# Forming half of the low weight parts with ScalarE and an accumulating DMA in both MLPs' first matrix

## The chip, the cores and the metric

The kernel runs on one core of one Trainium2 chip. The metric is device microseconds of one execution, from its first to its last instruction with the launch's own small overhead; two executions of the kernel before took 2568.08 and 2568.37 us, median 2568.22 us. Profiles are taken separately: one execution, recorded by the hardware.

The engines in the text are TensorE (PE in profile rows; its weight loads are PEld), VectorE (DVE), ScalarE (ACT), GpSimd (POOL) and the DMA queues that SyncE (SP) and GpSimd issue to. All DMA queues share the core's 16 DMA engines.

## The reference

A trunk of two layers on one sequence of 256 tokens, model width 2048, float32. Layer 0 is a retention layer, layer 1 is a latent attention (MLA) layer; each is followed by the same kind of MLP:

```python
def sq_relu_mlp(h, w1, w2):
    return jnp.square(jax.nn.relu(h @ w1)) @ w2

def reference(x, positions, ...):
    for layer in range(DEPTH):          # DEPTH = 2
        h = rms_norm(x, norm_mix[layer])
        if layer < N_A_LAYERS:          # layer 0
            x = x + retention(h, ...)
        else:                           # layer 1
            x = x + mla_attention(h, ...)
        x = x + sq_relu_mlp(rms_norm(x, norm_mlp[layer]), mlp_w1[layer], mlp_w2[layer])
    return x
```

The two matrices of an MLP are 2048 x 8192 (`w1`) and 8192 x 2048 (`w2`): 67 MB each in float32, so the two MLPs read 268 MB of the 470 MB that the kernel reads in all.

## The kernel before

**Two parts of a number.** Every product is made of three. A float32 matrix is split into a high part of 12 bits (`wh`, type fp32r) and a low part `wl = w - wh`; so are the activations. TensorE then adds high times high, high times low and low times high. `split` (L128) makes the parts: ScalarE copies the source into the high part, which rounds it (L131), and VectorE subtracts the rounded part from the source (L132).

**The stream of weights.** `stream` (L154) takes one chunk of a matrix, at most 128 partitions x 2048 float32, 1024 KB (1.05 million bytes). SyncE loads it into a buffer `raw`, of which there are three (L158). Each half of the chunk, 128 x 1024, is then split into one `wh` and one `wl` tile, of which there are five each; and `use` issues the matmuls on the half. The tile framework puts in the waits: a load waits until everything that read the `raw` buffer three chunks earlier is done, a split waits until TensorE is done with the tiles of five halves earlier.

**The first matrix of an MLP.** `gemm_t` (L201) makes 256 columns of `w1`, transposed, out of two chunks. For each block of 128 rows and each 128 columns it issues two matmuls: the low part of the weights against the 256 tokens' high activation (L216, 128 x 256), and the high part against the tokens' high and low activations side by side (L220, 128 x 512). After the second chunk `up` (L544) takes the 256 columns out of PSUM: ScalarE copies (L548), VectorE adds and applies relu and the norm's scale (L549, L551), ScalarE squares (L552), and a `split` makes the two parts of the hidden activations. The 8192 hidden features are made in three groups (of 12, 10 and 10 calls of `gemm_t`), and after each group the rows of `w2` that belong to it are multiplied in `gemm` (L191 to L194; three matmuls of 128 x 512 for each block). In profile rows the tiles of the first matrix are called `u_raw`, `u_wh`, `u_wl`, those of the second `d_raw`, `d_wh`, `d_wl`. One layer has 64 chunks of `u` and 64 of `d`.

**What sets the order.** Each engine works in the order of the program. ScalarE's queue in the first matrix has, for each chunk, two copies of a half, and after each second chunk the four steps of `up`. GpSimd's queue is empty in both MLPs but for the scales of the norm at their ends (`rstd`, L119 and L121). SyncE's queue has only the loads.

Of the kernel before, what the change touches and what calls it, by code (L numbers as in the profile page):

```python
# [15 lines left out]
AF = mybir.ActivationFunctionType  # L16
ALU = mybir.AluOpType
AX = mybir.AxisListType
PSUM = bass.MemoryType.PSUM
# [30 lines left out]
def yoco(ctx: ExitStack, tc: tile.TileContext, a):  # L50
# [19 lines left out]
        return psum.tile([P, 2, 512], F32, tag="at", bufs=1, name=name)  # L70

    def act_tile(name, dtype=F32R):
        """Two blocks of 128 features, each with its two halves (of precision, as a rule) side by side."""
        return pool.tile([P, 2, 2, S], dtype, tag="act", bufs=20, name=name)

    # Work that waits for other engines is issued some pieces of a product later.
    queue = []
    clock, count = [0], itertools.count()

# [14 lines left out]
        while len(items) < n:  # L94
            run_first()

# [1 line left out]
    gains = pool.tile([P, G_ALL], F32, name="gains")  # L98
    cst = pool.tile([P, C_ALL], F32, name="cst")
    pos_i = pool.tile([P, NT], I32, name="pos_i")  # L100
# [11 lines left out]
    def gain(col):  # L112
        return gains[:, col : col + 1]

# [1 line left out]
    def rstd(total, n, w, name):  # L116
        """(total / n + eps) ** -0.5 for [P, w] sums of squares."""
        m = small(w, f"{name}_m")
        nc.gpsimd.tensor_scalar(m, total, 1.0 / n, EPS, op0=ALU.mult, op1=ALU.add)  # L119
        r = small(w, f"{name}_r")  # L120
        nc.gpsimd.tensor_tensor(r, m, neg_half[:, :w], op=ALU.pow)  # L121
        return r
# [2 lines left out]
        junk = pool.tile([P, 512], BF16, tag="junk", bufs=2, name=f"{name}_sq")  # L125
        nc.scalar.activation(junk[:, : src.free_size()], src, AF.Square, accum_out=acc)

    def split(h, l, src, scale=None):  # L128
        """h + l = src * scale, each of 12 bits."""
        if scale is None:  # L130
            nc.scalar.copy(h, src)  # L131
            nc.vector.tensor_tensor(l, src, h.bitcast(F32), op=ALU.subtract)  # L132
        else:
            nc.scalar.activation(h, src, AF.Copy, scale=scale)  # L134
            nc.vector.scalar_tensor_tensor(
                l, src, scale, h.bitcast(F32), op0=ALU.mult, op1=ALU.subtract
            )
# [6 lines left out]
                split(v[:, j, 0], v[:, j, 1], src[:, j], scales[j])  # L144

    def transposed(srcs, name):
        """[tokens, 128] pairs of both token tiles -> [128, 2, S] in PSUM."""
        tp = bank("tp", [2, S], name)
        for j in range(2):
            for t in range(NT):  # L150
                nc.tensor.transpose(tp[:, j, t * P : (t + 1) * P], srcs(t, j), ident)
        return tp

    def stream(w, chunk, cols, name, use, done=None, before=None):  # L154
        """use(half, parts of the weights) for both halves of a chunk of the weights."""
        raw = pool.tile([P, 2048], F32, tag="raw", bufs=3, name=f"{name}_raw")
        if before is None:
            nc.sync.dma_start(raw[:, :cols], w[chunk])  # L158
        n = cols // 2
        for half in range(2):  # L160
            wh = pool.tile([P, 1024], F32R, tag="wh", bufs=5, name=f"{name}_wh{half}")
            wl = pool.tile([P, 1024], F32R, tag="wl", bufs=5, name=f"{name}_wl{half}")
            cuts = 1
            if before is not None:
                cuts = 1 if half else 2
                m = n // cuts
                for i in range(cuts):
                    lo = half * n + i * m
                    nc.sync.dma_start(raw[:, lo : lo + m], w[chunk][:, lo : lo + m])
                    if i == 0:  # L170
                        before(half)
            m = n // cuts
            for i in range(cuts):
                lo = half * n + i * m
                split(wh[:, i * m : (i + 1) * m], wl[:, i * m : (i + 1) * m], raw[:, lo : lo + m])
            use(half, wh, wl)
        if done is not None:
            queue.append((clock[0] + 1, -1, done))
        tick()

    def piece(w, chunk, acc, act, g, nk, nb, name, before=None, done=None):
        """acc[token tile] += act @ w for rows 512 * g to 512 * (g + 1)."""
        if before is None:
            need(act, 2 * g + 2)

        def use(half, wh, wl):
            for j in range(2):
                k = g * 4 + half * 2 + j
                rh, rl = (v[:, j * nb : (j + 1) * nb] for v in (wh, wl))
                for t in range(NT):  # L190
                    ah, al = (act[k // 2][:, j, i, t * P : (t + 1) * P] for i in range(2))  # L191
                    nc.tensor.matmul(acc[t], ah, rh, start=k == 0, stop=False)  # L192
                    nc.tensor.matmul(acc[t], ah, rl, start=False, stop=False)  # L193
                    nc.tensor.matmul(acc[t], al, rh, start=False, stop=k == nk - 1)  # L194

        stream(
            w, chunk, 4 * nb, f"{name}{g}", use, done and (lambda: done(acc)),
            before and (lambda half: before(2 * g + half)),
        )

    def gemm_t(w, chunk0, act, nk, name, done):  # L201
        """done(PSUM tiles [128 of 256 columns of w, (act parts h and l) @ w by token])."""
        acc = accs(512, name)
        n = nk // 8
        for g in range(n):
# [17 lines left out]
                        if k == 0:  # L223
                            low()

            stream(w, chunk0 + g, 2048, f"{name}{g}", use, (lambda: done(acc)) if g == n - 1 else None)

    def accs(nb, name):
        return [bank("acc", [nb], f"{name}_acc{t}") for t in range(NT)]

    def gemm(w, chunk0, act, nk, nb, name, done, before=None):
        """done(PSUM tiles [tokens, nb] of act @ w)."""
        acc = accs(nb, name)
        n = nk // 4
        for g in range(n - 1):
            piece(w, chunk0 + g, acc, act, g, nk, nb, name, before)
        last_piece(w, chunk0, acc, act, nk, nb, name, done, before)
# [3 lines left out]
        piece(w, chunk0 + g, acc, act, g, nk, nb, name, before, done)  # L241

    def gemm_blocks(w, chunk_of, act, nk, name, done):
        """All column blocks of 512, the first two side by side until the last rows of act."""
        n = nk // 4
        first = [accs(512, f"{name}{b}") for b in range(2)]
        for b in range(2):
            for g in range(n - 1):
                piece(w, chunk_of(b) + g, first[b], act, g, nk, 512, f"{name}{b}")
        for b in range(2):  # L250
            last_piece(w, chunk_of(b), first[b], act, nk, 512, f"{name}{b}", lambda acc, b=b: done(b, acc))
        for b in range(2, NB):
            gemm(w, chunk_of(b), act, nk, 512, f"{name}{b}", lambda acc, b=b: done(b, acc))

    def x_block_t(b, g0s, outs, name):
        """The split transposes of x's column block b, times each gain."""
        for k2 in range(2):
            tp = transposed(
                lambda t, j: x[t][b][:, (2 * k2 + j) * P : (2 * k2 + j + 1) * P], f"{name}_tp{b}{k2}"
# [20 lines left out]
    row = pool.tile([P, S], F32, name="row")  # L280

    def token_row(r, row, name):
        """row = the scales of the tokens, along every partition."""
        wide = f2k([NT, P], f"{name}_wide")
        for t in range(NT):
            nc.vector.tensor_copy(wide[:, t], r[t].to_broadcast([P, P]))
# [7 lines left out]
        later(1, turn)  # L294

    def into_next(ss, g0s, outs, r, name, row=None):
        """What follows a block of x that is complete; r gets the scales of the next norm."""

        def done(b, acc):
            add_to_x(acc, b, ss, name)  # L300
# [5 lines left out]

        return done

# [1 line left out]
    c1, c2, c3 = _pi_parts()  # L310
    pos_f = pool.tile([P, NT], F32, name="pos_f")

    def sincos(inv, w, name):
        """Makes what returns sin and cos [P, 2, NT, w] of position * inv."""
        n = NT * w
        ang = f2k([NT, w], f"{name}_ang")
        for t in range(NT):
# [70 lines left out]

        later(1, turn)

# [1 line left out]
    act0, r0, y_act, ret_sc, mla_sc = [], [], [], [], []  # L392

    def first_inputs(c):
        """The split columns 256 * c of the first norm's input."""
        t = f2k([2, S], f"x0t_{c}")
        nc.sync.dma_start(t, a["xt"][:, 2 * c : 2 * c + 2, :])
        v = act_tile(f"a0_{c}")
# [23 lines left out]
            later(20, mla_tables)  # L422

    def ret_rope(acc, out, name, wait):
        """One head's rotated q or k by feature: [128, dk half, S]."""
        u = f2k([2, S], f"{name}_u")
        for i in range(2):
            nc.scalar.copy(u[:, i], acc[i][:, S:])
# [106 lines left out]
        a["ret_w_out"], lambda b: b * 8, y_act, 32, "ro", into_next(ss, [G_MLP0], [act], r, "n1", row)  # L535
    )

# [1 line left out]
    def mlp(layer, act, row, done):  # L539
        w1, w2 = a[f"mlp_w1_{layer}"], a[f"mlp_w2_{layer}"]  # L540
        f0 = 0
        for gi, nf in enumerate(GROUPS):
# [12 lines left out]
                hid.append(v)  # L555

            for f in range(2 * f0, 2 * (f0 + nf)):
                gemm_t(w1, f * 2, act, KD, f"u{layer}_{f}", lambda acc, f=f: up(acc, f))
            for b in range(NB):

                def add(acc, b=b, last=gi == len(GROUPS) - 1):
# [10 lines left out]
    mlp(0, act, row, into_next(ss, [G_KV, G_MIX1], [act_kv, act_q], r2, "n2"))  # L572
    need(r2, 2)

# [1 line left out]
    def pe_rope(dst, u, src, t, i, heads):  # L576
        """dst = the rotation of src [P, heads, ROPE], gains in the tables."""

        def tab(j, lo, n):
            return pe_tabs[t][i][:, j, lo : lo + n].unsqueeze(1).to_broadcast([P, heads, n])  # L580
# [47 lines left out]
    for b in range(2):  # L628
        gemm(a[f"mla_w_kv_down_{b}"], 0, act_kv, KD, KV_NBS[b], f"kd{b}", lambda acc, b=b: downed(acc, b))

# [1 line left out]
    ssq = [small(3, f"ssq{t}") for t in range(NT)]  # L632
    cq, rq = [], []

# [21 lines left out]
    for b in range(3):  # L656
        gemm(a["mla_w_dq"], b * 4, act_q, KD, 512, f"dq{b}", lambda acc, b=b: queried(acc, b))

# [1 line left out]
    k_t, v_s = [], []  # L660

    def keyed(acc, b):
# [23 lines left out]
    for b in range(8):  # L686
        gemm(a["mla_w_kv_up"], b, ckv, 4, 512, f"ku{b}", lambda acc, b=b: keyed(acc, b))

# [1 line left out]
    nc.vector.tensor_scalar(gqn, gain(G_QN), scale, None, op0=ALU.mult)  # L690
    o_act = []

# [35 lines left out]
        later(3, turn)  # L728

    def score(b, qt, qpe):  # L730
        """Scores [query, head, keys of tile 0 for both query tiles, then tile 1], then softmax."""
        sc = two_banks(f"s{b}")
        for hh in range(2):
            rows = slice(hh * ROPE, (hh + 1) * ROPE)
# [145 lines left out]
```

## Time and profile before

| | |
|---|---|
| median of the executions shown | 2568.22 us |
| span of the profiled execution | 2566.0 us |
| matmul busy | 2554.7 us, 12786 matmuls |
| VectorE busy | 1475.5 us |
| ScalarE busy | 1233.7 us |
| GpSimd busy | 135.7 us |
| DMA | 473.85 MB, mean 185 GB/s |
| granted TensorE clock | 1.000 |

The profiled execution's own time is its span, 2566.0 us, with some 2 us around it up to the median of the timed executions. A row of the groups reads: line, engine, operation, output tile <- input tiles, shapes, count, then busy time and mean nanoseconds of one, then the engine's idle time before these instructions and what ended it. Matmuls are pipelined, so that the mean length of one is longer than the distance between two, and a busy TensorE is not TensorE at its peak. A DMA's row gives the time from its issue until its data has landed.

### The profile page before, as it was taken

To read this page: it belongs to the slowest core of one execution; us is meant where nothing else is said; L and a number is where in the kernel's file an instruction comes from. 1 tells how busy PE (TensorE), PEld (TensorE's weight loads), DVE (VectorE), ACT (ScalarE), POOL (GpSimd) and SP (SyncE) were. 2 spreads that over 40 slices of the span, in tenths; PEclk is the share of its full clock that TensorE was granted. 3 is DMA by queue.
4 is the path that set the end of the run, shared out by engine and by line. 5 is a ranking of instruction groups with operands and counts; after the bars stand their busy time and mean duration, and the time that the engine had idled before them with its cause. 6 is when DMAs were issued, how large, how long until landed. Compare 5 with 4: busy or idle time off the path is not lost.

```text
span 2566.0 us, 31690 instructions
## 1 busy us (share of the span) xinstructions
PE 2554.7 (100%) x12786; PEld 2168.1 (84%) x12786; DVE 1475.5 (58%) x1828; ACT 1233.7 (48%) x1651; POOL 135.7 (5%) x211
## 2 busy tenths in 40 slices
PE   8999999999999999999999999999999999999999
PEld 7888888888888888888888888998888888888887
DVE  6655555554556644654565656776666446645654
ACT  6444444443445533543454566554555435534542
POOL 6200000000000000000000002221000000000000
PEclk9999999999999999999999999999999999999999
DMA  8555555555555555555555464444455555555554
GB/s 297 182 177 180 181 181 183 182 184 186 190 183 192 183 197 194 184 188 191 196 182 196 148 221 152 148 144 148 174 188 182 196 197 181 191 190 193 184 202 140
DMA packets 71571, 473.85 MB, mean 185 GB/s; under 512 B 8192, under 2 KB 9344, under 8 KB 18176
## 3 DMA queue, kind: packets, MB, share of 16 engines
q1 hardware_dynamic: 71280, 471.78, 52.1%
q8 instruction: 100, 1.64, 0.2%
q14 instruction: 47, 0.39, 0.0%
q10 hardware_dynamic: 144, 0.05, 0.0%
HBM read 469.70 MB, written 2.10 MB: 184 GB/s over the span
## 4 chain that ended last, share of the span: by engine, by line
PE 97%; POOL 2%; DMA 0%; DVE 0%; issue 0%; SPq 0%; DVEq 0%
PE u_acc L220 19%; PE u_acc L216 9%; PE d_acc L192 9%; PE d_acc L194 9%; PE d_acc L193 9%; PE ro_acc L194 2%; PE ro_acc L193 2%; PE ro_acc L192 2%; PE rv_acc L192 2%; PE rv_acc L194 2%; PE rv_acc L193 2%; PE rk_acc L220 2%; PE rq_acc L220 2%; PE rg_acc L192 2%; PE rg_acc L194 2%; PE rg_acc L193 2%
## 5 line engine op out<-in xcount | busy, mean ns | idle before, releaser
L220 PE MATMUL u_acc<-n,u_wh 128*128 128x512 f32 x2048 | 718.1, 398 | 0.0
L216 PE MATMUL u_acc<-n,u_wl 128*128 128x256 f32 x2048 | 564.8, 281 | 0.0
L132 DVE TENSOR_TENSOR d_wl<-d_raw,d_wh 128x1024 fp32r<-128x1024 f32 x256 | 313.6, 1225 | 321.6 <-ACT d_wh L131 321.6
L220 PEld LDWEIGHTS u_acc<-n,u_wh 128*128 128x128 f32 x2048 | 381.0, 188 | 88.8
L132 DVE TENSOR_TENSOR u_wl<-u_raw,u_wh 128x1024 fp32r<-128x1024 f32 x256 | 313.3, 1224 | 241.1 <-ACT u_wh L131 241.1
L131 ACT CAST d_wh<-d_raw 128x1024 fp32r<-128x1024 f32 x256 | 269.8, 1054 | 374.0 <-PE d_acc L194 347.4
L192 PE MATMUL d_acc<-d_wh,hid 128*128 128x512 f32 x1024 | 398.6, 389 | 0.0
L194 PE MATMUL d_acc<-d_wh,hid 128*128 128x512 f32 x1024 | 398.4, 389 | 0.0
L193 PE MATMUL d_acc<-d_wl,hid 128*128 128x512 f32 x1024 | 398.4, 389 | 0.0
L131 ACT CAST u_wh<-u_raw 128x1024 fp32r<-128x1024 f32 x256 | 269.1, 1051 | 260.2 <-PE u_acc L220 210.2
L216 PEld LDWEIGHTS u_acc<-n,u_wl 128*128 128x128 f32 x2048 | 386.7, 189 | 5.6
L194 PEld LDWEIGHTS d_acc<-d_wh,hid 128*128 128x128 f32 x1024 | 192.3, 188 | 40.0
L193 PEld LDWEIGHTS d_acc<-d_wl,hid 128*128 128x128 f32 x1024 | 192.3, 188 | 39.8
L192 PEld LDWEIGHTS d_acc<-d_wh,hid 128*128 128x128 f32 x1024 | 192.3, 188 | 39.4
L132 DVE TENSOR_TENSOR ro_wl<-ro_raw,ro_wh 128x1024 fp32r<-128x1024 f32 x64 | 78.4, 1225 | 84.2 <-ACT ro_wh L131 84.2
L132 DVE TENSOR_TENSOR rg_wl<-rg_raw,rg_wh 128x1024 fp32r<-128x1024 f32 (+1 forms) x68 | 78.9, 1166 | 60.9 <-ACT rg_wh L131 60.9
L131 ACT CAST ro_wh<-ro_raw 128x1024 fp32r<-128x1024 f32 x64 | 67.4, 1053 | 94.6 <-PE ro_acc L194 86.5
L192 PE MATMUL rg_acc<-rg_wh,a 128*128 128x512 f32 x256 | 101.1, 396 | 5.7 <-ACT a L134 5.7
L132 DVE TENSOR_TENSOR rv_wl<-rv_raw,rv_wh 128x1024 fp32r<-128x1024 f32 x64 | 79.3, 1250 | 41.3 <-ACT rv_wh L131 41.3
L131 ACT CAST rg_wh<-rg_raw 128x1024 fp32r<-128x1024 f32 (+1 forms) x68 | 67.8, 998 | 72.9 <-PE rv_acc L194 46.7
L193 PE MATMUL rg_acc<-rg_wl,a 128*128 128x512 f32 x256 | 100.3, 392 | 0.2 <-DVE rg_wl L132 0.2
L192 PE MATMUL rv_acc<-rv_wh,a 128*128 128x512 f32 x256 | 100.4, 392 | 0.0
(260 smaller groups left out, 4072.5 us busy)
## 6 DMA issues: line engine op xcount, KB each, us to landing
u_raw<-in_mlp_w SPq DMA_DIRECT2D x128, 1024.0 KB, 4.8
d_raw<-in_mlp_w SPq DMA_DIRECT2D x128, 1024.0 KB, 4.8
rv_raw<-in_ret_w_gv SPq DMA_DIRECT2D x32, 1024.0 KB, 4.7
ro_raw<-in_ret_w_out SPq DMA_DIRECT2D x32, 1024.0 KB, 4.7
rg_raw<-in_ret_w_gv SPq DMA_DIRECT2D x28, 1024.0 KB, 4.7
uq_raw<-in_mla_w_uq SPq DMA_DIRECT2D x24, 768.0 KB, 4.3
rq_raw<-in_ret_w_qk SPq DMA_DIRECT2D x16, 1024.0 KB, 4.8
rk_raw<-in_ret_w_qk SPq DMA_DIRECT2D x16, 1024.0 KB, 4.7
```

Source lines behind the costliest of these rows:

```text
L131: nc.scalar.copy(h, src)
L132: nc.vector.tensor_tensor(l, src, h.bitcast(F32), op=ALU.subtract)
L192: nc.tensor.matmul(acc[t], ah, rh, start=k == 0, stop=False)
L193: nc.tensor.matmul(acc[t], ah, rl, start=False, stop=False)
L194: nc.tensor.matmul(acc[t], al, rh, start=False, stop=k == nk - 1)
L216: nc.tensor.matmul(acc[f][:, 0:S], wl[:, cols], a[:, 0], start=False, stop=False)
L220: nc.tensor.matmul(acc[f], wh[:, cols], a.rearrange("p i s -> p (i s)"), start=k == 0, stop=k == nk - 1)
```

## The change

`mlp` passes its layer's number to `gemm_t`, and this to `stream`, as `dma_low`. For the second half of each chunk of `w1`, and for nothing else, `split` then works in another way: ScalarE writes the high part as before, ScalarE writes minus the source rounded to the same type, which is minus the high part, into the low part's tile, and a DMA issued by GpSimd adds the float32 weights to that tile in place. The DMA's source is the weights in HBM in layer 0 (`dma_low` is 0, `w[chunk]`), and the `raw` buffer in SBUF in layer 1 (`dma_low` is 1). VectorE has no part in these halves any more. There are 64 such halves in each layer. Comments were taken out as well, and line numbers move by a few.

```diff
-    def split(h, l, src, scale=None):
-        if scale is None:
+    def split(h, l, src, scale=None, again=None):
+        if again is not None:
+            nc.scalar.copy(h, src)
+            nc.scalar.activation(l, src, AF.Copy, scale=-1.0)
+            nc.gpsimd.dma_start(l, again, accum_op=ALU.add)
+        elif scale is None:
             nc.scalar.copy(h, src)
             nc.vector.tensor_tensor(l, src, h.bitcast(F32), op=ALU.subtract)
...
-    def stream(w, chunk, cols, name, use, done=None, before=None):
+    def stream(w, chunk, cols, name, use, done=None, before=None, dma_low=None):
...
-                split(wh[:, i * m : (i + 1) * m], wl[:, i * m : (i + 1) * m], raw[:, lo : lo + m])
+                part = slice(lo, lo + m)
+                again = None
+                if dma_low is not None and half == 1:
+                    again = (raw if dma_low else w[chunk])[:, part]
+                split(wh[:, i * m : (i + 1) * m], wl[:, i * m : (i + 1) * m], raw[:, part], again=again)
...
-    def gemm_t(w, chunk0, act, nk, name, done):
+    def gemm_t(w, chunk0, act, nk, name, done, dma_low=None):
...
-            stream(w, chunk0 + g, 2048, f"{name}{g}", use, (lambda: done(acc)) if g == n - 1 else None)
+            stream(
+                w, chunk0 + g, 2048, f"{name}{g}", use, (lambda: done(acc)) if g == n - 1 else None, dma_low=dma_low
+            )
...
-                gemm_t(w1, f * 2, act, KD, f"u{layer}_{f}", lambda acc, f=f: up(acc, f))
+                gemm_t(w1, f * 2, act, KD, f"u{layer}_{f}", lambda acc, f=f: up(acc, f), dma_low=layer)
```

## The prediction, before the result was known

> **What bounds the kernel now.** I read the page's busy times first, then the chain that ended last, then the waits of TensorE, and then one stretch of the first matrix in order of time.
>
> ```profile
> PE 2554.7 (100%) x12786; PEld 2168.1 (84%) x12786; DVE 1475.5 (58%) x1828; ACT 1233.7 (48%) x1651; POOL 135.7 (5%) x211
> ...
> PE 97%; POOL 2%; DMA 0%; DVE 0%; issue 0%; SPq 0%; DVEq 0%
> ...
> L132 DVE TENSOR_TENSOR u_wl<-u_raw,u_wh 128x1024 fp32r<-128x1024 f32 x256 | 313.3, 1224 | 241.1 <-ACT u_wh L131 241.1
> ```
> ```profile
> PE rg_acc L192 <- ACT a L134: 5.7, 1, 5.7
> PE tr_tp L151 <- DVE tr_scaled L384: 1.1, 2, 0.7
> PE rg_acc L193 <- DVE rg_wl L132: 0.2, 1, 0.2
> ```
>
> TensorE is the bound everywhere. The chain is 97% TensorE, and the second fence is the whole list of what TensorE waited for: three entries, 7.0 us, all at the start and none in an MLP. The change can gain nothing that the chain holds: all of TensorE's idle time is 2566.0 - 2554.7 = 11.3 us. The 128 subtractions that VectorE loses (128 x 1.224 = 157 us) lie beside matmuls. So the question is only whether the new way of making a low part still arrives in time.
>
> The stretch that tells is one turn of ScalarE in the first matrix (columns: start, length, operation, idle before and its releaser):
>
> ```profile
> 1250.28 0.73 ACT L548 COPY u<-u_acc 128x256 f32<-128x256 f32 x2 [1.43 <-PE u_acc L220]
> 1250.90 1.05 ACT L131 CAST u_wh<-u_raw 128x1024 fp32r<-128x1024 f32 x1
> 1252.22 0.63 ACT L552 ACTIVATE u<-u 128x512 f32<-128x512 f32 x1 [0.27 <-DVE u L551]
> 1252.88 0.62 ACT L131 CAST hid<-u 128x512 fp32r<-128x512 f32 x1
> 1253.44 1.05 ACT L131 CAST u_wh<-u_raw 128x1024 fp32r<-128x1024 f32 x1
> 1256.26 1.05 ACT L131 CAST u_wh<-u_raw 128x1024 fp32r<-128x1024 f32 x1 [1.77 <-PE u_acc L220]
> 1259.09 1.05 ACT L131 CAST u_wh<-u_raw 128x1024 fp32r<-128x1024 f32 x1 [1.77 <-PE u_acc L220]
> 1261.56 0.73 ACT L548 COPY u<-u_acc 128x256 f32<-128x256 f32 x2 [1.43 <-PE u_acc L220]
> ...
> 1267.55 1.05 ACT L131 CAST u_wh<-u_raw 128x1024 fp32r<-128x1024 f32 x1 [1.77 <-PE u_acc L220]
> ```
>
> From 1250.28 to 1261.56 is one call of `gemm_t`, two chunks, four halves: 11.28 us, so **5.64 us for a chunk and 2.82 for a half**. The casts at 1253.44 and 1259.09 are those of second halves, which the change touches. Each starts as TensorE gives back the tile of five halves earlier, so TensorE has four halves in hand, 4 x 2.82 = 11.28 us, before it needs this one. Before the change 1.05 + 1.22 us of it are used.
>
> **The change part by part.**
>
> *ScalarE.* 128 more instructions of 128 x 1024. No row has this form; the 128 x 512 rows above give 0.63 for ACTIVATE beside 0.62 for CAST, so I take 1.07, a little over the cast's 1.05 (bounds 1.05, and twice 0.63, 1.27). 128 x 1.07 = 137 us. They lie in ScalarE's idle time: the first between 1254.49 and 1256.26 (1.77 us), the second between 1260.14 and 1261.56 (1.42 us). Were that cover gone, `up`'s copies would start a fraction of a microsecond later, against a whole call of 11.28 us until their PSUM tiles are wanted again: nothing. The second write waits for the low tile of five halves earlier, which TensorE gives back no later than the high one; behind it in ScalarE's queue stand the next cast and `up`, and they lose nothing by it.
>
> *GpSimd.* 128 issues. No row shows GpSimd issuing a DMA. The near rows:
>
> ```profile
> L158 SPq DMA_DIRECT2D u_raw<-in_mlp_w x128: 327/328/328, 728.6 to 2424.4; - x128
> ```
> ```profile
> L119 POOL TENSOR_SCALAR n_m<-n_tot 128x1 f32<-128x1 f32 x8 | 2.4, 302 | 981.4 <-DVE n_tot L270 981.0
> ...
> L327 POOL TENSOR_TENSOR tr_kl<-tr_k,tr_kh 128x512 f32<-128x512 f32 x1 | 2.4, 2369 | 0.1
> ...
> L121 POOL TENSOR_TENSOR cq_r<-cq_m,neg_half 128x1 f32<-128x1 f32 x2 | 2.1, 1044 | 0.2
> ```
>
> SyncE's issue takes 0.33 us, GpSimd's dearest single operation 2.37. I take 1.0, the price of a small GpSimd operation that does work for each partition, and keep both ends. One issue in 5.64 us fits either way. An issue that waits holds up only the issues behind it and, at the end of an MLP, the norm's scales (L119), which come after the last matrix block and so long after the last add. [...]
>
> *The add itself.* No row has an accumulating DMA. The nearest are plain loads:
>
> ```profile
> u_raw<-in_mlp_w SPq DMA_DIRECT2D x128, 1024.0 KB, 4.8
> ...
> x<-in_x SPq DMA_DIRECT2D x8, 256.0 KB, 8.6
> ...
> kd_raw<-in_mla_w_kv_down SPq DMA_DIRECT2D x4, 512.0 KB, 3.3
> ```
>
> Twice the bytes take 1.5 us more, so a load is 1.8 us and 1.5 for each 512 KB. The lower end for the add is 3.3. It must read the tile as well as the weights, twice the bytes in, and I take the 1024 KB row, **4.8**. The upper end, however far, is the slowest rate of the three rows, 8.6 for 256 KB, hence 17.2; those loads were queued behind others at the kernel's start. [...] With the write counted as a third pass the row would be 1.8 + 4.5 = 6.3, and that case is a rival below.
>
> What the 16 engines can carry is seen where loads are queued (columns: stretch, busy times, then clock, DMA share, GB/s):
>
> ```profile
> 20.00:24.00 4.00, 4.00 (x19) 3.31 (x18) 4.00 (x6) 3.28 (x7) 3.83 (x3) 1.00 1.03 416
> 24.00:28.00 4.00, 4.00 (x19) 3.16 (x18) 4.00 (x6) 2.42 (x4) 3.85 (x3) 1.00 1.02 411
> 28.00:32.00 4.00, 4.00 (x22) 3.40 (x21) 2.52 (x2) 2.15 (x6) 3.83 (x3) 1.00 1.02 412
> 32.00:36.00 4.00, 4.00 (x25) 3.45 (x24) 2.78 (x2) 4.00 (x9) 3.83 (x3) 1.00 1.02 415
> 1250.28:1306.73 56.45, 56.45 (x322) 49.04 (x321) 34.89 (x40) 30.09 (x41) 0.00 (x0) 1.00 0.53 186
> ```
>
> About 415 GB/s with the engines full, and 186 in the first matrix. With the add as two reads a chunk moves 1.05 + 1.05 = 2.10 million bytes in 5.64 us, 372 GB/s, nine tenths of 415: it fits, and load and add will overlap most of the time. Where they overlap wholly, the two take 2.10 MB / 415 GB/s = 5.05 us of data, and each lands 1.8 + 5.05 = 6.85 us after its issue.
>
> *Layer 0 (weights from HBM).* The negative is ready at 1253.44 + 1.05 + 1.07 = 1255.56. TensorE ends halves 2.82 apart, at 1250.62 (2.82 and 5.64 before the releases of 1253.44 and 1256.26), so the half five later begins at 1250.62 + 5 x 2.82 = 1264.72: a cover of **9.16 us** for issue and landing. Alone these take 1.0 + 4.8 = 5.8, fully overlapped 7.85. Hidden. The raw buffer is given back by ScalarE at 1255.56, where VectorE did it at 1253.44 + 1.05 + 1.22 = 1255.71; the next load into it is due at 1267.55, 12 us later, and even at 6.85 is in time. Without the cover a microsecond too much costs a third of one for each chunk, since the ring of five tiles comes round in three chunks: 64 / 3 = 21 us for the layer.
>
> *Layer 1 (weights from the raw buffer).* Here the buffer is held until the add has landed, and only then SyncE may load the chunk three later. The wait that is late next is SyncE's, and behind it stand all later loads. From 1255.56 to the cast of that buffer at 1267.55 is 12.0 us for add plus load: 5.8 + 4.8 = 10.6 alone, 7.85 + 6.85 = 14.7 fully overlapped. A late cast can be caught up, since the three ScalarE steps then run on end, 1.05 + 1.05 + 1.07 = 3.17; three chunks are 16.92, so add plus load may be 13.75 before TensorE pays. At 10.6 it pays nothing; at 14.7 the chunk takes (14.7 + 3.17) / 3 = 5.96, 0.32 more, 64 x 0.32 = 20 us. The engines are nine tenths full, which speaks for the late end, and a late load overlaps less, which speaks for the early one: I take the middle, **10 us**.
>
> Sum: nothing from VectorE and ScalarE, 0 in layer 0, +10 in layer 1: span 2566.0 + 10 = 2576, and with the 2.2 us that lie between span and median **2578 us**. At the issue's upper end, 2.37, layer 0 stands at its edge (9.2) and layer 1 at (16.1 + 3.17) / 3 = 6.42, +50; at the add's lower end nothing is paid, 2568.
>
> **The rivals.** About 2% (51 us) is what a measurement of this kernel can tell from no change.
>
> *The engines fill up, slower.* The place is the 16 DMA engines in the first matrix. They carry 5.64 x 415 = 2.34 MB in a chunk, so the add may cost 1.29 MB, 2.5 times its 0.524 MB. At three passes (read, read, write) a chunk is 2.62 MB, 6.32 us: 128 x 0.68 = +87, **2655 us**. At four it is 7.58, +249, 2817. For it: nothing in the trace says that an engine adds as fast as it copies. Against it: the 415 rows count a load's bytes once although it is read and written.
>
> *The add is late, with the engines not full.* If issue and landing take 12 us, layer 0's ring gives 3 chunks = 5.64 + 2.12 + 12, 6.59 for one, +61; layer 1's (12 + 4.8 + 3.17) / 3 = 6.66, +65: **2694 us**. For it: the 8.6 us of the 256 KB row, and that GpSimd's price is unknown. Against it: the 3.3 of the 512 KB row.
>
> *The freed VectorE helps.* At most TensorE's 11.3 us of idle time, which lie elsewhere: 2557.
>
> **How the numbers follow.** The forecast (0 to 50 us more, all within 2%) has 0.51, the full engines 0.28, the late add 0.20 (a quarter of it short of 51 us), the gain 0.01. That gives within 2% 0.51 + 0.05 + 0.01 = 0.57, less 0.01 kept for a gain that no row shows: 0.56; slower 0.28 + 0.15 = 0.43; faster 0.01. The range goes from 2565 to 2760: it leaves out the dearer 0.15 of the full engines and hardly anything below, and takes in the late add.
>
> **What would show it.** GpSimd's 128 issues and their landing: near 6 to 8 us, in both layers. ScalarE's new row near 1.07, VectorE's `u_wl` row with 128 instead of 256. DMA share in the first matrix near 0.9 to 1.0, with GB/s up. No wait of TensorE for the add in layer 0, a few tenths a chunk in layer 1, and there SyncE's wait ended by the add. Wrong it would be if the add lands later than 9 us even in layer 0, or if the engines' share is 1 at fewer than 372 GB/s.

## The result

The changed kernel took 2594.59 us (2589.93 and 2599.24) against 2568.22 us: a ratio of 1.0103, 95% interval 1.0084 to 1.0122. A second measurement gave 2590.05 us, 1.0088 (1.0073 to 1.0103). It is slower, by about 1%, where 2578 was forecast: the sign and the 2% bound were right, the size about two fifths of what came. The profiled execution has a span of 2597.5 us, 31.5 more than before; it is the longer of the two executions.

On the page after the change, these lines answer to those shown of before (busy times, the chain, the groups of the new low parts, the DMA queues):

```profile
PE 2562.7 (99%) x12786; PEld 2170.2 (84%) x12786; DVE 1319.6 (51%) x1700; ACT 1348.9 (52%) x1779; POOL 246.7 (9%) x339
...
q1 hardware_dynamic: 71280, 471.78, 50.3%
q0 software_dynamic: 18432, 67.12, 14.0%
...
PE 73%; issue 14%; DMA 9%; POOL 3%; ACT 1%; DVE 0%; SPq 0%; POOLq 0%; ACTq 0%; DVEq 0%
...
L132 ACT ACTIVATE u_wl<-u_raw 128x1024 fp32r<-128x1024 f32 x128 | 135.4, 1058 | 77.5 <-PE u_acc L224 60.4
...
L133 POOL DMA_DIRECT2D u_wl<-in_mlp_w x64 | 55.6, 869 | 712.5 <-ACT u_wl L132 700.3
...
L133 POOL DMA_DIRECT2D u_wl<-u_raw x64 | 55.2, 863 | 644.7 <-ACT u_wl L132 543.0
```

The pieces cost about what was put down for them: ScalarE's write 1.06 us (1.07), GpSimd's issue 0.86 (1.0), and VectorE lost 156 us of work that nobody waited for. What is new is DMA in the chain, and these waits of TensorE and of its weight loads (columns: time in all, times, longest):

```profile
PE u_acc L224 <- DMA u_wl<-u_raw: 12.2, 9, 2.9
PE u_acc L224 <- DMA u_wl<-in_mlp_w: 11.8, 14, 2.0
```
```profile
PEld u_acc L224 <- DMA u_wl<-in_mlp_w: 18.0, 20, 2.4
PEld u_acc L224 <- DMA u_wl<-u_raw: 15.9, 12, 3.2
```

TensorE waits for the add in both layers (`in_mlp_w` is layer 0, `u_raw` layer 1; the two lists overlap in time). How the loss divides is read from the tile `row`, which is written once at the start of each MLP. Before, then after:

```profile
L292 ACT COPY row<-n_rtp x2: 367/367/367, 761.0 to 1861.9; 128x256 f32<-128x256 f32 x2
```
```profile
L302 ACT COPY row<-n_rtp x2: 362/362/363, 760.5 to 1877.3; 128x256 f32<-128x256 f32 x2
```

Between the two copies lie layer 0's MLP and the attention: 1100.9 us before, 1116.8 after, +15.9. Behind the second copy lies layer 1's MLP: 704.1 us before, 720.2 after, +16.1. (The stretch ahead of the first copy is 0.5 shorter.) **Both layers pay alike** in this execution, where 0 and 10 had been forecast.

The issues and their landings (size, then median us from issue to landing):

```profile
u_raw<-in_mlp_w SPq DMA_DIRECT2D x128, 1024.0 KB, 7.9
...
u_wl<-in_mlp_w POOLq DMA_DIRECT2D x64, 512.0 KB, 10.0
u_wl<-u_raw POOLq DMA_DIRECT2D x64, 512.0 KB, 7.7
```

The add lands 10.0 us after its issue in layer 0, not 7.85 at the most. And one stretch of the first matrix in each of two groups (columns as before; the last three are clock, DMA share, GB/s):

```profile
1030.00:1120.00 90.00, 88.20 (x499) 75.83 (x498) 36.05 (x48) 61.45 (x79) 13.12 (x16) 1.00 1.00 272
```
```profile
1250.00:1260.00 10.00, 9.98 (x57) 8.41 (x57) 2.36 (x4) 6.41 (x8) 1.73 (x2) 1.00 1.02 282
1260.00:1270.00 10.00, 8.10 (x38) 6.79 (x37) 3.01 (x4) 4.29 (x6) 0.86 (x1) 0.83 1.00 273
```

The DMA engines show a share of 1.00. The second fence shows that a stall can cost twice: TensorE is idle for 1.9 us between 1260 and 1270, and its granted clock there is 0.83, which is another 1.7. In slices of 2 us the clock reads 0.91, 0.50 and 0.73 from 1262 to 1268, and 1.00 on both sides. Two waits in layer 1, of 2.9 and 2.6 us, were followed by the same drop (0.67, 0.50 and 0.98 from 2188 to 2194, and 0.84, 0.50 and 0.81 from 2416 to 2422); the other waits were not, though one of them, in layer 0, took 2.0. Each drop lost 1.7 us. Three times 1.7 are about 5 of the 31.5 us, and over the execution the clock was 0.998. What decides whether a wait is followed by a drop these traces do not tell: after 1.9, 2.6 and 2.9 us one came, after 2.0 none.

### The profile page after: what moved, and what is told of

Read it like the earlier page. It is cut to its first block, busy times and chain, and to the rows that moved or that the text cites. A ratio compares the mean times of both kernels' runs of the same rounds, so it can differ in the third digit from the quotient of the medians.

```text
span 2597.5 us, 32181 instructions
## 1 busy us (share of the span) xinstructions
PE 2562.7 (99%) x12786; PEld 2170.2 (84%) x12786; DVE 1319.6 (51%) x1700; ACT 1348.9 (52%) x1779; POOL 246.7 (9%) x339
## 3 DMA queue, kind: packets, MB, share of 16 engines
q0 software_dynamic: 18432, 67.12, 14.0%
## 4 chain that ended last, share of the span: by engine, by line
PE 73%; issue 14%; DMA 9%; POOL 3%; ACT 1%; DVE 0%; SPq 0%; POOLq 0%; ACTq 0%; DVEq 0%
PE d_acc L200 7%; PE d_acc L201 7%; PE d_acc L202 7%; PE u_acc L228 6%; DMA u_wl<-u_raw 4%; PE u_acc L224 3%; DMA u_raw<-in_mlp_w 3%; PE ro_acc L202 2%; PE ro_acc L200 2%; PE ro_acc L201 2%; PE rv_acc L200 2%; PE rv_acc L202 2%; PE rv_acc L201 2%; DMA u_wl<-in_mlp_w 2%; PE rk_acc L228 2%
## 5 line engine op out<-in xcount | busy, mean ns | idle before, releaser
L136 DVE TENSOR_TENSOR u_wl<-u_raw,u_wh 128x1024 fp32r<-128x1024 f32 x128 | 156.6, 1223 | 297.3 <-ACT u_wh L135 297.3
L132 ACT ACTIVATE u_wl<-u_raw 128x1024 fp32r<-128x1024 f32 x128 | 135.4, 1058 | 77.5 <-PE u_acc L224 60.4
L559 DVE TENSOR_TENSOR u<-u_acc,u 128x256 f32<-128x256 f32 x128 | 49.4, 423 | 158.3 <-ACT u L558 158.3
L133 POOL DMA_DIRECT2D u_wl<-in_mlp_w x64 | 55.6, 869 | 712.5 <-ACT u_wl L132 700.3
L133 POOL DMA_DIRECT2D u_wl<-u_raw x64 | 55.2, 863 | 644.7 <-ACT u_wl L132 543.0
```

The costliest lines, as they stand in the source:

```text
L132: nc.scalar.activation(l, src, AF.Copy, scale=-1.0)
L133: nc.gpsimd.dma_start(l, again, accum_op=ALU.add)
L559: nc.vector.tensor_tensor(u[:, i], acc[i][:, 0:S], u[:, i], op=ALU.add)
```

## The experiments

Two readings were open. The DMA engines could be full, so that load and add together set the pace (A). Or the engines could carry both, and the add, landing late in a crowd, is later than the rings of buffers cover (B, later D). That ScalarE's further writes delay the casts was a third (C).

**Without the add**, without its addition, with a smaller load. Three edits:

```diff
-            nc.gpsimd.dma_start(l, again, accum_op=ALU.add)                        # no_add
...
-            nc.gpsimd.dma_start(l, again, accum_op=ALU.add)                        # copy_not_add
+            nc.gpsimd.dma_start(l, again)
...
-            nc.sync.dma_start(raw[:, :cols], w[chunk])                             # half_load
+            n_load = cols if dma_low is None else cols // 2
+            nc.sync.dma_start(raw[:, :n_load], w[chunk][:, :n_load])
...
-                    again = (raw if dma_low else w[chunk])[:, part]
+                    again = raw[:, 0:m] if dma_low else w[chunk][:, part]
+                    part = slice(0, m)
```

> The DMA of the add is left out; ScalarE still writes high and negative, so the low parts of the second halves are minus the high parts. Theory A (the DMA engines are full with load and add): no add, nothing to wait for, 2566 to 2572 us. Theory B (the add lands too late for the rings of buffers, whatever the engines do): the same, 2566 to 2572. Theory C (ScalarE's 128 further writes delay the casts): most of the +26 stays, 2585 or more.

> GpSimd's DMA copies the weights over the tile and does not add, so the low parts of the second halves are the weights. One read less per byte, all waits and buffers the same. Theory A: engine time of this DMA falls from 2.8 us to about 1.5 for each engine, share in the first matrix near 0.78, landing 4 to 6.5 us, time 2566 to 2574. Theory B (late because GpSimd issues it and because of the way, not because of the bytes): landing stays above 8 us, time 2580 or more.

> The first matrix loads only half of each chunk, 512 KB, and takes both halves from it (the second half of each chunk of the weights is left out; the add stays 512 KB from HBM in layer 0 and from the raw buffer in layer 1). Theory A: the engines have 1.5 us less to do in each chunk, share near 0.75, the adds land in 5 to 6.5 us, 2566 to 2574. Theory B: the adds land as late as before, 8 to 10 us, and at least layer 0 keeps its 16 us, 2582 or more.

Measured: 2567.53 us without the add (0.9997, 0.9987 to 1.0006), 2567.92 with the copy (0.9999, 0.9990 to 1.0008), 2568.36 with half the load (1.0003, 0.9994 to 1.0012). So C falls: ScalarE's 128 writes, with GpSimd's issues and waits kept in the copy, cost nothing. The whole loss hangs on the second read of the add beside a whole load. The landings of the copy's kernel, then of half the load:

```profile
u_raw<-in_mlp_w SPq DMA_DIRECT2D x128, 1024.0 KB, 6.2
...
u_wl<-in_mlp_w POOLq DMA_DIRECT2D x64, 512.0 KB, 4.9
u_wl<-u_raw POOLq DMA_DIRECT2D x64, 512.0 KB, 5.0
```
```profile
u_raw<-in_mlp_w SPq DMA_DIRECT2D x128, 512.0 KB, 5.7
...
u_wl<-in_mlp_w POOLq DMA_DIRECT2D x64, 512.0 KB, 7.0
u_wl<-u_raw POOLq DMA_DIRECT2D x64, 512.0 KB, 6.0
```

Both read 1.57 million bytes a chunk in place of 2.10, and their DMAs land in 7 us or less, by the median. By the view's count of bytes the copy moves 281 GB/s, where the add moved 272, and takes a smaller share of the engines (0.82 in the stretch that had 1.00):

```profile
1030.00:1120.00 90.00, 90.00 (x512) 78.20 (x511) 35.93 (x48) 62.99 (x80) 8.44 (x16) 1.00 0.82 281
```

For these two runs B had been put down as a lateness of the way itself, whatever the bytes, with landings of 8 us or more and times of 2580 or more. That was wrong on both counts: the landing follows the crowd, though with half the load it stayed above A's 5 to 6.5 in layer 0. Whether the engines are full (A) or carry the crowd and land it late (what is left of B) these runs do not tell. The median landing of the copy is alike from HBM (4.9) and from SBUF (5.0).

**Wider rings.** Six tiles each of the high and the low part; six low tiles alone; four raw buffers; four raw buffers with six low tiles. Where room was needed, it comes from scratch tiles that no MLP holds in such number (not shown in the diff):

```diff
-            wh = pool.tile([P, 1024], F32R, tag="wh", bufs=5, name=f"{name}_wh{half}")
-            wl = pool.tile([P, 1024], F32R, tag="wl", bufs=5, name=f"{name}_wl{half}")
+            wh = pool.tile([P, 1024], F32R, tag="wh", bufs=6, name=f"{name}_wh{half}")   # six_tiles
+            wl = pool.tile([P, 1024], F32R, tag="wl", bufs=6, name=f"{name}_wl{half}")   # six_tiles, six_low, four_raw_six_low
...
-        raw = pool.tile([P, 2048], F32, tag="raw", bufs=3, name=f"{name}_raw")
+        raw = pool.tile([P, 2048], F32, tag="raw", bufs=4, name=f"{name}_raw")           # four_raw, four_raw_six_low
```

> Six tiles each for high and low parts in place of five (room made by one junk tile and six small ones less, which no MLP uses in number): 2.8 us more cover for the add. Theory A: the engines stay full, layer 0 keeps its loss of 16 us or nearly, and layer 1, whose ring goes by the three raw buffers, keeps its own: 2588 to 2600. Theory B: layer 0 has 12 us of cover for a landing of 10 and loses nothing, layer 1 keeps 16: 2580 to 2585.

> Six low tiles, high tiles and raw buffers as in the changed kernel. Theory D (layer 0 pays by the ring of five low tiles): the negative may start once ScalarE is past the cast of the half before, some 1.8 us earlier, cover near 12 us against landings of 10: layer 0 loses 0 to 3 us; layer 1 keeps 5 to 16 by its raw buffers: 2573 to 2585. If layer 0 pays by its high tiles or by raw loads that come late: it keeps 10 or more, 2587 to 2600.

> Four raw buffers in place of three, tiles as in the changed kernel (room made by one junk tile and six small ones less). Theory D (load and add share the engines and both land late, 9 to 10 us; layer 0 pays by the ring of five tiles, layer 1 by the ring of three raw buffers): layer 0 keeps its 16 us; in layer 1 SyncE no longer waits for the add to the last, loads and adds overlap as in layer 0, so the add's landing rises from 7.7 to 9 or more and the ring of five tiles takes over: it loses 5 to 16 us. In all 2587 to 2600. Theory E (the add from the raw buffer is the faster one by its source): its landing stays below 8 and layer 1 loses nothing, in all 2580 to 2586.

> Four raw buffers and six low tiles (five high ones; two scratch tiles of 2 KB, one junk tile and six small ones less). Theory D: both rings are wide enough, landings stay at 9 to 10 us in both layers and cost nothing: 2566 to 2574. If the engines themselves were the limit (share 1.0 in the first matrix): 2590 or more, as without.

| kernel | median us | ratio (95%) | profiled span over before's | ahead of the MLPs | layer 0 | layer 1 |
|---|---|---|---|---|---|---|
| changed | 2594.59 | 1.0103 (1.0084 to 1.0122) | +31.5 | -0.5 | +15.9 | +16.1 |
| changed, again | 2590.05 | 1.0088 (1.0073 to 1.0103) | +25.7 | -0.4 | +10.9 | +15.2 |
| six tiles | 2574.52 | 1.0033 (1.0019 to 1.0047) | +6.7 | +2.0 | +1.5 | +3.2 |
| six low tiles | 2571.92 | 1.0019 (1.0009 to 1.0028) | +7.5 | +0.2 | +0.3 | +7.0 |
| four raw | 2578.72 | 1.0042 (1.0028 to 1.0056) | +22.0 | -0.4 | +15.8 | +6.6 |
| four raw, six low | 2568.65 | 1.0003 (0.9993 to 1.0012) | +2.5 | +0.8 | +0.3 | +1.4 |

The last three columns are worked out as above from each profile's `row`, those of six tiles, of six low tiles, of four raw, and of both. They hold for the one execution that was profiled; executions of the kernel before lie up to 3 us apart, so that 1 or 2 us in these columns say nothing.

```profile
L302 ACT COPY row<-n_rtp x2: 367/368/368, 763.0 to 1865.4; 128x256 f32<-128x256 f32 x2
```
```profile
L302 ACT COPY row<-n_rtp x2: 367/367/367, 761.2 to 1862.4; 128x256 f32<-128x256 f32 x2
```
```profile
L302 ACT COPY row<-n_rtp x2: 361/361/361, 760.6 to 1877.3; 128x256 f32<-128x256 f32 x2
```
```profile
L302 ACT COPY row<-n_rtp x2: 366/366/366, 761.8 to 1863.0; 128x256 f32<-128x256 f32 x2
```

A falls. In the profiled executions one more low tile takes away layer 0's whole loss, four raw buffers leave it whole and take away most of layer 1's. With both, the kernel is back at the time of before in every one of its ten executions (2567.35 to 2570.28). The engines do the same work meanwhile. This is the same stretch of layer 0 with six tiles, and the landing of its add, 9.7 us where it was 10.0:

```profile
1030.00:1120.00 90.00, 90.00 (x513) 78.21 (x512) 36.46 (x49) 61.44 (x80) 13.81 (x16) 1.00 1.01 280
```
```profile
u_wl<-in_mlp_w POOLq DMA_DIRECT2D x64, 512.0 KB, 9.7
```

The share is 1.01 and TensorE is busy throughout. So a share of 1.0 is no sign of full engines, and an add that lands nearly as late costs nothing when the ring covers it. Layer 1 has two rings that bind: either one widened leaves 3 to 7 us, and with both widened what is left, 1.4, is within the spread.

Not all of it came as expected. Six tiles came out below the ranges of both theories, because layer 1 gained too, and six low tiles just below theirs. With six low tiles the add of layer 0 also landed earlier, after 8.5 us (8.3 with four raw buffers as well, where 9 to 10 was expected):

```profile
u_wl<-in_mlp_w POOLq DMA_DIRECT2D x64, 512.0 KB, 8.5
```

ScalarE writes the negative earlier there, so that the next load is issued 1.6 us behind the add in place of 0.7. It is the run with six tiles, then, that shows the cover by itself. With four raw buffers layer 1's add was to land after 9 us or more by D, and its landing stayed at 7.5:

```profile
u_wl<-in_mlp_w POOLq DMA_DIRECT2D x64, 512.0 KB, 10.1
u_wl<-u_raw POOLq DMA_DIRECT2D x64, 512.0 KB, 7.5
```
```profile
SPq L162 <- DMA u_wl<-u_raw: 358.4, 64, 10.5
```

SyncE still waits for an add before each of its 64 loads in layer 1 (364.6 us with three buffers). A load there is issued when an add has landed, so the two meet less than in layer 0. E had put the shorter landing down to the source. Against it: the adds of layer 1 in the changed kernel land between 4.5 and 10.5 us, the dearest as late as layer 0's median, and layer 1 still lost 6.6 us with four raw buffers, where E had nothing. No run has an add from HBM alone on the engines, so a part of the source is not ruled out. The median of four raw, 2578.72, lies below both ranges, while its profiled execution, with a span of 2588.0, was the longest of its five; how much layer 0 lost in the other four no profile shows.

**The layers changed about.**

```diff
-                gemm_t(w1, f * 2, act, KD, f"u{layer}_{f}", lambda acc, f=f: up(acc, f), dma_low=layer)
+                gemm_t(w1, f * 2, act, KD, f"u{layer}_{f}", lambda acc, f=f: up(acc, f), dma_low=1 - layer)
```

> Layer 0 adds from the raw buffer and layer 1 from HBM. Theory D: the layers change places and the time stays, 2588 to 2600; the layer that adds from HBM shows a landing of 10 and SyncE waiting for ScalarE and VectorE, the other one 7.5 to 8 and SyncE waiting for the add. If it is the layer and not the source or the held buffer, layer 0 keeps 10.

2594.08 us, 1.0096 (1.0081 to 1.0111), and the landings go with the way of the add and not with the layer. By its `row` layer 0 lost 17.5 us and layer 1 11.0:

```profile
u_wl<-u_raw POOLq DMA_DIRECT2D x64, 512.0 KB, 7.4
...
u_wl<-in_mlp_w POOLq DMA_DIRECT2D x64, 512.0 KB, 9.8
```
```profile
L302 ACT COPY row<-n_rtp x2: 362/363/364, 760.2 to 1878.6; 128x256 f32<-128x256 f32 x2
```

**Twice and half as many adds.**

```diff
-                if dma_low is not None and half == 1:
+                if dma_low is not None:                                # all_halves
...
-                if dma_low is not None and half == 1:
+                if dma_low is not None and half == 1 and chunk % 2:    # every_second
```

> Both halves of each chunk of the first matrix get their low part from ScalarE and the add: twice the adds. Reads of load and adds are 1.05 + 2.10 = 3.15 million bytes a chunk. If about 415 GB/s of reads is what the engines carry: 7.6 us a chunk in place of 5.64, 128 x 1.95 = +250, about 2820. If the engines' time by packets adds up (2.9 for a load, 2.84 for an add): 8.6 us, +378, about 2945. The rings can only add to either.

> Only the second chunk of each pair gets the add, half as many adds (64). Reads are 1.57 million bytes a chunk on average, 279 GB/s. Theory D: an add is alone with loads for 11.3 us, lands in 6 to 8 us, within the cover of five tiles, 2566 to 2573. If it is the share of halves alone that counts and not the room on the engines: half of the loss, 2578 to 2584.

With all halves: 2820.71 us, 1.0984 (1.0962 to 1.1006), the first of the two expectations. 252.5 us over 128 chunks are 1.97 us each, 7.61 us a chunk, and 3.15 million bytes in 7.61 us are 413 GB/s: the 411 to 416 of queued loads before the change. Here the engines are full, with a share (1.02) hardly higher than that of six tiles (1.01):

```profile
1050.00:1150.00 100.00, 83.14 (x423) 66.86 (x421) 13.72 (x23) 62.22 (x74) 23.36 (x27) 0.98 1.02 272
```

The GB/s of this view count an add's bytes once (on the page after the change q0 holds 67.12 MB for 128 adds of 0.524); 272 x 3.15 / 2.10 = 408 is read. By the same count six tiles read 280 x 2.10 / 1.57 = 373, nine tenths of it. That an add is paid by its two reads, as the prediction took it, agrees with this: with the write counted as a third pass the engines would have carried 4.19 / 7.61 = 551 GB/s, more than any row shows.

With every second chunk: 2567.54 us, 0.9998 (0.9989 to 1.0007), no loss. Its adds show the price by itself, as minimum, median and maximum; first in the last group of layer 0 (the first two have medians of 8.1 and 8.6), then of layer 1:

```profile
DMA to landing us min/median/max: 8.0/8.0/8.8
```
```profile
DMA to landing us min/median/max: 4.5/4.6/5.2
```

In layer 0 ScalarE's negative releases the add and its high part, the write behind it, the next load, which is issued 0.7 us after the add; the two meet: 8.0. In layer 1 the load waits for the add, which meets only the end of the load before it: 4.6.

## Why the prediction was right in sign and short in size

- **ScalarE, GpSimd, VectorE**: right. Nothing was lost with the add's DMA left out (0.9997).
- **The add's price**: right in kind, two reads (so counted, all halves read 413 GB/s, the 411 to 416 of queued loads), and high for the add nearly alone: 1.0 + 4.8 = 5.8 was put down, 4.6 measured (from the raw buffer). Met by one load, 7.85 was put down, 8.0 to 8.6 measured.
- **"Where they overlap wholly ... each lands 6.85 us after its issue"**: this is the term that was mis-sized. With issue it made 7.85 the upper end for the add in the changed kernel; it was 10.0, and the load beside it took 9.3 in place of 6.85 (the loads of layer 0's second group, minimum, median, maximum):

```profile
DMA to landing us min/median/max: 7.9/9.3/10.4
```

  The step let one add meet one load. But a load that takes longer than the 5.64 us from one to the next also meets the following add, and that one the load after it. With loads of 9.3 us there is always one in flight, and each add meets two.
- **Layer 0's cover**: 9.16 us from the negative was put down. ScalarE turned out to write the negative ahead of the high part, against the order of the source lines, which gives 1.05 us more, and GpSimd starts 0.30 us after it:

```profile
1066.50 1.06 ACT L132 ACTIVATE u_wl<-u_raw 128x1024 fp32r<-128x1024 f32 x1 [1.50 <-PE u_acc L224]
1067.47 1.03 ACT L131 CAST u_wh<-u_raw 128x1024 fp32r<-128x1024 f32 x1
```
```profile
1067.86 0.86 POOL L133 DMA_DIRECT2D u_wl<-in_mlp_w  x1 [4.46 <-ACT u_wl L132]
```

  From issue to TensorE's need that leaves 11.28 - 1.06 - 0.30 = 9.92 us. The median landing, 10.0, stands at this edge, so the later ones stall TensorE's weight loads, up to 2.4 us at a time. "Hidden" became +10.9 to +15.9, and with a sixth tile +0.3.
- **Layer 1's ring of raw buffers**: right as a mechanism, +10 put down, +15.2 and +16.1 measured. It was not alone: the ring of low tiles binds there too, for a sixth low tile alone brings the layer's loss down to +7.0.
- **The rival of the full engines** was rightly put below the forecast. It decides at 2.34 million bytes a chunk: the kernel with wide rings, at 2.10, lies below that point and pays nothing, and the kernel with all halves, at 3.15, lies above it and pays in full. The rival of the late add had the mechanism of layer 0, at 10 us in place of its 12.
- **What was to make it wrong** came, both signs of it. The add landed later than 9 us in layer 0. And the share was 1.00 where the engines read 272 x 2.10 / 1.57 = 363 GB/s, under 372; six tiles show that this second sign does not tell full engines. The forecast's 0 to 50 us more still held the time, because the adds were late only now and then: TensorE waited for 14 of the 64 in layer 0 and for 9 in layer 1, 24 us in all. The sign was not luck, for layer 1's loss, the only one put down, would have given it alone. That the whole stayed within the 50 us was in part: about half of it came from layer 0, which was called hidden.

## What to carry to other kernels

A transfer that is hidden when alone must be priced at the utilization it makes itself. Here, near nine tenths of what the engines carry, landings about doubled (the load's from 4.8 to 9.3 us; the add's to 10.0, where it took 4.6 nearly alone and from the raw buffer), and the cover of a ring of buffers is to be held against the late landings and not against the mean. Whether the busy DMA was the pace or only late was told here by one more buffer (a sixth low tile took layer 0 from +15.9 to +0.3), not by its share (1.01 with six tiles, 1.02 with all halves). And work moved off an engine that nobody waited for could only cost: the best version found, with four raw buffers and six low tiles, is back at the time of before (2568.65 us, 1.0003) and no faster.

## What the runs showed beside it

- A DMA share of 1.00 to 1.02 stands for 373 GB/s of reads in one kernel and for 408 in another; the room between them does not show in it.
- A stall of TensorE can cost nearly as much again in granted clock, as between 1260 and 1270 (1.9 us idle, 1.7 by the clock of 0.83), but only three of the 23 waits for an add were followed by such a drop; in the profile of four raw buffers and six low tiles the clock is 1.000 over the span.
- The same kernel loses 10.9 us in layer 0 in one execution and 15.9 in another, while the kernel before has executions within 3 us of each other. A landing at the edge of its cover would turn small differences into stalls; that is a reading and not shown, and which difference it is stays open.
